# Attention in a two-layer hybrid block: probabilities times values as float32 matmuls, two heads side by side in the array's columns, row sums added up on GpSimd

## The chip, the cores and the metric

The kernel runs on one core of one Trainium2 chip. The metric is device time of one execution in microseconds, as the median of several runs. The core has five engines that take their instructions in order: TensorE (PE, with its weight loads shown apart as PEld), VectorE (DVE), ScalarE (ACT), GpSimd (POOL) and SyncE (SP, which issues the DMA transfers here).

## The reference

Two layers work on 512 latent tokens and 256 context tokens of width 1024. The first mixes tokens by multi-head latent attention with 16 heads, the second by a Hyena convolution; each is followed by a gated ConvFFN. Only the output of the latent tokens is returned, so the context matters as keys and values of the attention. The part that the change touches is, in the reference:

```python
    def one_block(qblk):
        s = jnp.einsum('bqhd,bkhd->bhqk', qblk, k).astype(F32) * scale
        p = jax.nn.softmax(s, axis=-1).astype(v.dtype)
        return jnp.einsum('bhqk,bkhd->bqhd', p, v)
```

All data are float32. There are 512 queries and 768 keys, 96 numbers in a query or key of a head and 64 in a value.

## The kernel before

Matmuls are made as products of split numbers. A float32 number is cut into a high part, rounded to the type float32r, and a low part, the rest; `mm3` (L137 to L139) adds three float32r matmuls, high by high, high by low and low by high. Weights are split on arrival by ACT (L129) and DVE (L130). A few small products use float32 operands as they are: the column sums and broadcasts of the norms (L247, L296), and the modulation rows of `Mods.rows` (L168). The latter puts four matmuls with 32 stationary columns each into four column groups of the array, by writing to partitions 0, 32, 64 and 96 of one PSUM tile `modp`.

The attention works on pairs of heads: `p` is the pair, `kt` a block of 128 of the 768 keys (six blocks), `b` the head of the pair. All is held with keys on the partitions and the 512 queries along the row.

- `s_step` makes the scores of a block with three float32r matmuls (tile `s`), then the exponentials twice, as float32r (`ph`) and as float32 (`pf`), on ACT; the difference `pl` is made on POOL or DVE by turns (L754, L756).
- `v_step` multiplies by the values. `split_v` has cut the values `vf` into `vh` (64 columns and two of ones, so that the row sums of the exponentials come out as rows 64 and 65) and `vl`. Three matmuls for each head and block, L768, L769 and L771, go to a PSUM tile for each head, `po0` and `po1`. After the last block ACT copies sums and results out (`sm`, `ou`), and the sums go by DMA through DRAM, a reciprocal on DVE (L781) and a broadcast back as `rb`; `normalize` multiplies (L793) and splits the result into `oh` and `ol` for the projection (`pj`).
- `side` weaves the preparation of the next pair in between: keys (`pk`), queries (`pq`, `rot`), and the largest scores, which are found by a float32r product of the high parts (`sm` written by L728, 384 columns, into the one tile that DVE's maximum L730 reads) and turned into a row by four small matmuls with one stationary column (`mr`, L735).

What stands in the code is not the order in which an engine runs it: the framework's scheduler orders each engine's instructions when the program is built, so that a matmul of `side` may stand between two matmuls of one `v_step`.

Of the kernel before, what the change touches and what calls it, by code (L numbers as in the profile page):

```python
# [17 lines left out]
P = 128  # L18
D = 1024
NC = D // P  # L20
T = 512
TC = 256
TK = T + TC
HEADS = 16
# [6 lines left out]
ATT_SCALE = 1.0 / math.sqrt(96.0)  # L31
# [26 lines left out]
def hybrid_kernel(ctx, tc, A, out):  # L58
    nc = tc.nc
    dma = nc.sync.dma_start  # L60
    act = nc.scalar.activation
    stt = nc.vector.scalar_tensor_tensor
    vtt = nc.vector.tensor_tensor
    vts = nc.vector.tensor_scalar
    mm = nc.tensor.matmul
# [40 lines left out]
    ones = gp.tile([P, P], F32, name="ones")  # L106
# [241 lines left out]
                              hh[:, j, c], hl[:, j, c], self.tmp, self.n)  # L348
            return hh, hl

# [1 line left out]
    def sin_of(ps, b, f, pool, outt, n):  # L352
        a = pool.tile([P, T], F32, tag="ff", name="sa", bufs=2)[:, :n]
        r = pool.tile([P, T], F32, tag="ff", name="sn", bufs=2)[:, :n]
# [106 lines left out]
                        if kt:  # L461
                            between()

# [182 lines left out]
    def attention(ab, L):  # L646
        at, cosq, sinq, cqh, cql = (L[n] for n in ("at", "cos", "sin", "cqh", "cql"))
        kb = L["kb"] + [(ab.tile([P, TK], F32R, name=f"kh{i}"), ab.tile([P, TK], F32R, name=f"kl{i}")) for i in (2, 3)]
        qb = [(ab.tile([P, T], F32R, name=f"qh{i}"), ab.tile([P, T], F32R, name=f"ql{i}")) for i in range(4)]
        vb = [(ab.tile([P, 6, 2, 66], F32R, name=f"vh{i}"), ab.tile([P, 6, 2, 64], F32R, name=f"vl{i}")) for i in range(2)]  # L650
        for vh, _ in vb:
            for b in range(2):
                nc.vector.tensor_copy(out=vh[:, :, b, 64:66], in_=ones[:, 0:12].rearrange("p (k o) -> p k o", o=2))

        wq = {0: tuple(wcols(w, 4, 384) for w in L["wuq"])}

# [7 lines left out]
        vf = {}  # L664

        def load_v(p):
            vf[p] = ab.tile([P, 6, 2, 64], F32, tag="vf", name="vf", bufs=1)
            dma(out=vf[p].rearrange("p k b d -> p k (b d)"), in_=vst[p // 4][p % 4])

        def split_v(p):  # L670
            vh, vl = vb[p % 2]
            nc.scalar.copy(out=vh[:, :, :, 0:64], in_=vf[p])
            nc.gpsimd.tensor_tensor(out=vl, in0=vf[p], in1=vh[:, :, :, 0:64], op=ALU.subtract)

        def gemm_q(g, r):
            pe = pst("pq")
# [4 lines left out]

        def prod_rope(g, meanwhile=None):
            pe = gemm_q(g, 0)
            ph = ab.tile([P, T], F32R, tag="ph", name="rph", bufs=5)
            pl = ab.tile([P, T], F32R, tag="pl", name="rpl", bufs=5)
# [6 lines left out]
            sb = ab.tile([P, T], F32, tag="ou", name="rsb", bufs=1)  # L692
# [45 lines left out]
        pts = {}  # L738

        def s_step(h, kt):  # L740
            kh, kl = kb[h % 4]
            qh, ql = qb[h % 4]
            ks = slice(kt * P, kt * P + P)
            s = pst("s")
            mm(s, lhsT=kh[0:97, ks], rhs=qh[0:97], start=True, stop=False)
            mm(s, lhsT=kh[0:96, ks], rhs=ql[0:96], start=False, stop=False)
            mm(s, lhsT=kl[0:96, ks], rhs=qh[0:96], start=False, stop=True)
            pf = at.tile([P, T], F32, tag="wv", name="pf", bufs=4)
            ph = ab.tile([P, T], F32R, tag="ph", name="ph", bufs=5)
            pl = ab.tile([P, T], F32R, tag="pl", name="pl", bufs=5)  # L750
# [10 lines left out]
        def v_step(p, kt):  # L761
            if kt == 0:
                pos[p] = (pso("po0"), pso("po1"))
            P2 = [pts.pop((2 * p + b, kt)) for b in range(2)]
            vh, vl = vb[p % 2]
            f, l = kt == 0, kt == 5
# [3 lines left out]
            for b in range(2):  # L770
                mm(pos[p][b][:66], lhsT=vh[:, kt, b, :], rhs=P2[b][1], start=False, stop=l)  # L771
            if l:
                ou = ab.tile([P, T], F32, tag="ou", name="ou", bufs=1)
                sm = at.tile([P, T], F32, tag="wv", name="sm", bufs=4)
                for b in range(2):
                    nc.scalar.copy(out=sm[32 * b:32 * b + 2], in_=pos[p][b][64:66])
                    dma(out=rst[0][p][b:b + 1, :], in_=sm[32 * b:32 * b + 1])
                    nc.scalar.copy(out=ou[64 * b:64 * b + 64], in_=pos[p][b][:64])
# [9 lines left out]
        norm = []  # L788

        def normalize():  # L790
            while norm:
# [7 lines left out]
        prod_rope(0, lambda: prod_q(0))  # L799
        for t in (1, 2):  # L800
            L["prod_v"](1, t)
        split_v(0)
# [19 lines left out]
        def side(n, i):  # L822
            if i == 11 and n % 2 and n + 1 < NP:
                prod_rope((n + 1) // 2)
            if n >= NP:
                return
            if i == 0:
                put_rope(n)
                if n > 1:
                    prod_k(n, 0, kb, L)  # L830
            elif i == 1 and n > 1:
                prod_k(n, 1, kb, L)
            elif i == 2:
                if n > 1:
                    prod_q(n)
                if n % 2 and n // 2 + 1 < 4:
                    load_wq(n // 2 + 1)
            elif 2 < i < 11:
                max_step(2 * n + (i - 3) // 4, (i - 3) % 4)
                if i == 6 or i == 10:  # L840
                    max_row(2 * n + (i == 10))
                if i == 9:
                    split_v(n)
                    if n + 1 < NP:
                        load_v(n + 1)

        pend = []
        for p in range(NP):
            for kt in range(6):
                for b in range(2):  # L850
                    s_step(2 * p + b, kt)
                    side(p + 1, 2 * kt + b)
                    if b == 1 and len(pend) == 2:
                        v_step(*pend.pop(0))
                if kt == 2:
                    normalize()
                pend.append((p, kt))
        while pend:
            v_step(*pend.pop(0))
        normalize()  # L860
        return oh, ol

# [1 line left out]
    def project(x, rh, rl, wname, gl, nm, mid, extra, bname=None):  # L864
        bg = None
        if bname:
# [71 lines left out]
                        if half:  # L938
                            nm.add(x[:, q, c], h)

# [1 line left out]
    def hyena(hh, hl):  # L942
        with tc.tile_pool(name="hy", bufs=1, side="left", reuse_waits="tile") as hy:
            yf = hy.tile([P, NC, T], F32, name="yf")
# [152 lines left out]
            split_y(range(6, 8))  # L1097
        return yh, yl

# [1 line left out]
    atx = ExitStack()  # L1101
    oh, ol = mla()
    atx.close()
# [171 lines left out]
```

## Time and profile before

| | |
|---|---|
| time, median of 3 runs | 1461.13 us (1460.64 to 1461.48) |
| span of the profiled execution | 1459.7 us |
| PE busy in it | 1395.5 us (96%) |
| DVE, ACT, POOL busy | 975.7, 615.9, 205.8 us |
| mean granted clock of PE | 0.986 |

The span runs from the first to the last instruction on the core; the profiled execution's own time is not given apart from it, and the 1.4 us between its span and the median of the runs is what lies around a span. Matmuls are pipelined and the end of each is modelled, so a matmul's listed duration overlaps with the next one's; the time from one start to the next is what a matmul costs in a dense stretch. The attention, from the first exponentials to the start of the projection, lies at about 187 to 394 us.

### The profile page before, as it was taken

How to read it: one execution, taken by the hardware profiler on the slowest of the kernel's cores; microseconds unless marked ns; L12 is line 12 of the kernel's file. 1: busy time of each engine (PE TensorE's matmuls, PEld its weight loads, DVE VectorE, ACT ScalarE, POOL GpSimd, SP SyncE). 2: the span in 40 equal slices, each digit the busy share in tenths (PEclk: the TensorE clock that was granted, in tenths of full speed). 3: DMA queues.
4: the chain of work that ended last, by engine and by line, in shares of the span. 5: the costliest groups of instructions: out<-in, count | busy, mean ns of one | idle time of the engine just before them, and what ended most of it. 6: DMA issues, size and time to landing. Idle time of an engine off the chain costs nothing. (4 is left out here: it accounts for less than half of the span.)

```text
span 1459.7 us, 17476 instructions
## 1 busy us (share of the span) xinstructions
PE 1395.5 (96%) x6766; PEld 1111.5 (76%) x6766; DVE 975.7 (67%) x1471; ACT 615.9 (42%) x965; POOL 205.8 (14%) x168
## 2 busy tenths in 40 slices
PE   5899899999999999999999999999899999999997
PEld 2577677766688878787878987887798888888886
DVE  5875676677467877657764688889786653355545
ACT  5444478678724433224342352323344432234420
POOL 4401124323330000000001103331310000000011
PEclk9999999999999999999999999999999999999998
DMA  9672511113162754665523342122313223332121
GB/s 367 218 272 96 150 33 59 41 55 113 45 228 96 234 189 164 235 233 183 181 89 112 141 164 104 68 85 86 134 70 115 78 68 104 116 112 78 60 79 58
DMA packets 46670, 186.58 MB, mean 128 GB/s; under 512 B 5320, under 2 KB 17864, under 8 KB 32380
## 3 DMA queue, kind: packets, MB, share of 16 engines
q1 hardware_dynamic: 46588, 185.48, 37.0%
q8 instruction: 53, 0.87, 0.2%
q14 instruction: 29, 0.24, 0.0%
HBM read 171.29 MB, written 11.60 MB: 125 GB/s over the span
## 5 line engine op out<-in xcount | busy, mean ns | idle before, releaser
L129 ACT CAST wh<-wr 128x1024 fp32r<-128x1024 f32 (+2 forms) x209 | 195.4, 955 | 180.8 <-PE dn L138 89.0
L130 DVE TENSOR_TENSOR wl<-wr,wh 128x1024 fp32r<-128x1024 f32 (+2 forms) x209 | 242.4, 1175 | 24.3 <-ACT wh L129 21.2
L267 POOL TENSOR_TENSOR sqa<-sqa,sq 128x512 f32<-128x512 f32 (+1 forms) x42 | 58.2, 1386 | 837.1 <-ACT sq L265 836.1
L139 PE MATMUL dn<-gh,wl 128*128 128x512 f32 (+1 forms) x396 | 146.8, 371 | 0.0
L137 PE MATMUL dn<-gh,wh 128*128 128x512 f32 (+1 forms) x396 | 146.7, 372 | 0.0
L138 PE MATMUL dn<-gl,wh 128*128 128x512 f32 (+1 forms) x396 | 146.3, 369 | 0.0
L318 DVE SCALAR_TENSOR_TENSOR z<-ua,vec,z 128x511 f32<-128x511 f32 x44 | 33.0, 750 | 109.9 <-ACT z L317 109.8
L934 DVE SCALAR_TENSOR_TENSOR x<-dn,modc,x 128x512 f32<-128x512 f32 (+1 forms) x36 | 24.9, 691 | 109.4 <-PE dn L139 109.4
L317 ACT ACTIVATE z<-ua,vec 128x512 f32<-128x512 f32 x44 | 34.3, 780 | 149.2 <-PE ua L139 149.2
L137 PEld LDWEIGHTS dn<-gh,wh 128*128 128x128 f32 x396 | 74.4, 188 | 15.6 <-ACT wh L129 0.8
L138 PEld LDWEIGHTS dn<-gl,wh 128*128 128x128 f32 x396 | 74.5, 188 | 14.3
L139 PEld LDWEIGHTS dn<-gh,wl 128*128 128x128 f32 x396 | 74.4, 188 | 13.9
L137 PE MATMUL hz<-hyh,wh 128*128 128x512 f32 (+1 forms) x224 | 82.2, 368 | 0.0
L139 PE MATMUL hz<-hyh,wl 128*128 128x512 f32 (+1 forms) x224 | 81.9, 366 | 0.0
L754 POOL TENSOR_TENSOR pl<-pf,ph 128x512 fp32r<-128x512 f32 x48 | 63.0, 1318 | 133.3 <-ACT pf L752 132.0
L138 PE MATMUL hz<-hyl,wh 128*128 128x512 f32 (+1 forms) x224 | 81.7, 365 | 0.0
L901 ACT ACTIVATE sg<-z 128x512 f32<-128x512 f32 x44 | 27.8, 633 | 109.6 <-DVE z L319 104.4
L137 PE MATMUL ua<-hf1h,wh 128*128 128x512 f32 (+1 forms) x192 | 72.5, 378 | 1.1 <-ACT hf1h L307 1.1
L138 PE MATMUL ua<-hf0l,wh 128*128 128x512 f32 (+1 forms) x192 | 72.9, 380 | 0.4 <-DVE hf0l L308 0.4
L137 PE MATMUL ua<-hf0h,wh 128*128 128x512 f32 (+1 forms) x192 | 73.1, 381 | 0.0
L138 PE MATMUL ua<-hf1l,wh 128*128 128x512 f32 (+1 forms) x192 | 72.6, 378 | 0.5 <-DVE hf1l L308 0.5
L139 PE MATMUL ug<-hf0h,wl 128*128 128x512 f32 (+1 forms) x192 | 73.0, 380 | 0.0
(388 smaller groups left out, 3572.7 us busy)
## 6 DMA issues: line engine op xcount, KB each, us to landing
wr<-in_wup SPq DMA_DIRECT2D x44, 1024.0 KB
mw<-in_modw SPq DMA_DIRECT2D x40, 1024.0 KB
wr<-in_wdn SPq DMA_DIRECT2D x32, 704.0 KB
wr<-in_win SPq DMA_DIRECT2D x12, 1024.0 KB
mw<-in_modw SPq DMA_DIRECT2D x16, 512.0 KB
fspec<-fs SPq DMA_DIRECT2D x16, 256.0 KB
wr<-in_wo SPq DMA_DIRECT2D x4, 1024.0 KB
fq<-fspec SPq DMA_DIRECT2D x8, 512.0 KB
```

The source lines that it names most:

```text
L129: nc.scalar.copy(out=wh[:, c], in_=wr[:, c])
L130: vtt(out=wl[:, c], in0=wr[:, c], in1=wh[:, c], op=ALU.subtract)
L137: mm(ps, lhsT=ah, rhs=bh, start=first, stop=False)
L138: mm(ps, lhsT=ah, rhs=bl, start=False, stop=False)
L139: return mm(ps, lhsT=al, rhs=bh, start=False, stop=last)
L267: nc.gpsimd.tensor_tensor(out=acc, in0=acc, in1=sq, op=ALU.add)
L317: act(out=z, in_=p, func=AF.Identity, bias=b, scale=w1)
L318: stt(out=z[:, 1:T], in0=p[:, 0:T - 1], scalar=w0, in1=z[:, 1:T], op0=ALU.mult, op1=ALU.add)
L754: nc.gpsimd.tensor_tensor(out=pl, in0=pf, in1=ph, op=ALU.subtract)
L901: act(out=sg, in_=zs[1], func=AF.Silu)
L934: i = stt(out=x[:, q, c], in0=job[0][:, c], scalar=mcol(l, 5, q), in1=x[:, q, c], op0=ALU.mult, op1=ALU.add)
```

## The change

The values are no longer split and the exponentials are made once, as float32. `v_step` is called for two blocks at a time, and makes one float32 matmul for each head and block: the first head of a pair writes to partitions 0 to 63 of one PSUM tile `po`, the second to 64 to 127, which puts them in the two halves of the array's columns. The row sums no longer come from columns of ones: the exponentials of a head are added up into a tile `acc` (on POOL, the last four on DVE), and `row_sums` multiplies it by a float32 tile of ones, 32 columns for each head of the pair. Buffers change too: `pf` has a tag of its own with eight, `vf` and `ou` have two.

```diff
-        def split_v(p):
-            vh, vl = vb[p % 2]
-            nc.scalar.copy(out=vh[:, :, :, 0:64], in_=vf[p])
-            nc.gpsimd.tensor_tensor(out=vl, in0=vf[p], in1=vh[:, :, :, 0:64], op=ALU.subtract)
...
-            act(out=ph, in_=s, func=AF.Exp, scale=ATT_SCALE)
             act(out=pf, in_=s, func=AF.Exp, scale=ATT_SCALE)
-            if (h + kt) % 2 == 0:
-                nc.gpsimd.tensor_tensor(out=pl, in0=pf, in1=ph, op=ALU.subtract)
+            pts[h, kt] = pf
+            if kt == 0:
+                return
+            if kt == 1:
+                accs[h] = ab.tile([P, T], F32, tag="acc", name="acc", bufs=4)
+                prev = pts[h, 0]
             else:
-                vtt(out=pl, in0=pf, in1=ph, op=ALU.subtract)
-            pts[h, kt] = (ph, pl)
+                prev = accs[h]
+            add = vtt if h >= HEADS - 2 and kt > 3 else nc.gpsimd.tensor_tensor
+            add(out=accs[h], in0=prev, in1=pf, op=ALU.add)
...
-            for b in range(2):
-                mm(pos[p][b][:66], lhsT=vh[:, kt, b, :], rhs=P2[b][0], start=f, stop=False)
-                mm(pos[p][b][:64], lhsT=vl[:, kt, b, :], rhs=P2[b][0], start=False, stop=False)
-            for b in range(2):
-                mm(pos[p][b][:66], lhsT=vh[:, kt, b, :], rhs=P2[b][1], start=False, stop=l)
...
+        def v_step(p, kts):
+            if kts[0] == 0:
+                pos[p] = pso("po")
+            for kt in kts:
+                for b in range(2):
+                    mm(pos[p][64 * b:64 * b + 64], lhsT=vf[p][:, kt, b, :], rhs=pts.pop((2 * p + b, kt)),
+                       start=kt == 0, stop=kt == 5)
+            if kts[-1] == 5:
+                ou = ab.tile([P, T], F32, tag="ou", name="ou", bufs=2)
+                nc.scalar.copy(out=ou, in_=pos.pop(p))
+                ends.append((p, ou))
...
+        def row_sums():
+            while ends:
+                p, ou = ends.pop(0)
+                rsum = pst("rsum")
+                for b in range(2):
+                    mm(rsum[32 * b:32 * b + 32], lhsT=ones[:, 0:32], rhs=accs.pop(2 * p + b), start=True, stop=True)
                 sm = at.tile([P, T], F32, tag="wv", name="sm", bufs=4)
+                nc.scalar.copy(out=sm[0:64], in_=rsum[0:64])
...
-                if kt == 2:
+                if kt % 2 == 0 and pend:
+                    v_step(*pend.pop(0))
+                if kt == 1:
+                    row_sums()
+                if kt == 4:
                     normalize()
-                pend.append((p, kt))
+                if kt % 2:
+                    pend.append((p, (kt - 1, kt)))
```

Where the instructions come to stand on PE is the scheduler's doing. The first place is the product of one step with the values in the third pair of heads; a row is a line of the code, the tile written from the tiles read, and columns by row length. Before, the six matmuls of a block stand so, with a product of `side` among them:

```order
L768 MATMUL po_1664<-ph,vh_1354 66x512
L728 MATMUL sm<-kh_612,qh_1346 128x384 x2
L769 MATMUL po_1664<-ph,vl_1355 64x512
L768 MATMUL po_1665<-ph,vh_1354 66x512
L769 MATMUL po_1665<-ph,vl_1355 64x512
L771 MATMUL po_1664<-pl,vh_1354 66x512
L771 MATMUL po_1665<-pl,vh_1354 66x512
```

In the changed kernel the four matmuls of two blocks stand so (heads alternate from one to the next; line 719 is `side`'s product, 736 to 738 the scores):

```order
L738 MATMUL s<-qh_1352,kl_1345 128x512
L759 MATMUL po<-pf,vf 64x512 x3
L719 MATMUL sm<-kh_612,qh_1346 128x384 x2
L759 MATMUL po<-pf,vf 64x512
L736 MATMUL s<-qh_1350,kh_1342 128x512
```

The four are cut into a run of three and a run of one by a product that fills all 128 columns. The whole order has 45 runs of `po`: 2 of four matmuls, 22 of three, 1 of two and 20 of one, 96 matmuls in all.

The second place is the row sums of the same pair, which did not stand on PE before:

```order
L738 MATMUL s<-qh_1352,kl_1345 128x512
L773 MATMUL rsum<-acc,ones 32x512
L719 MATMUL sm<-kh_612,qh_1346 128x384 x2
L773 MATMUL rsum<-acc,ones 32x512
L736 MATMUL s<-qh_1350,kh_1342 128x512
```

The two heads' sums are parted by the same kind of product. There are 14 runs of `rsum`: 12 of one matmul and 2 of two, the last of them right behind the last run of `po`.

## Rows read from the trace of the kernel before

**Rows 1.** The page: PE's busy time; GpSimd's float32 addition.

```profile
PE 1395.5 (96%) x6766; PEld 1111.5 (76%) x6766; DVE 975.7 (67%) x1471; ACT 615.9 (42%) x965; POOL 205.8 (14%) x168
...
L267 POOL TENSOR_TENSOR sqa<-sqa,sq 128x512 f32<-128x512 f32 (+1 forms) x42 | 58.2, 1386 | 837.1 <-ACT sq L265 836.1
```

**Rows 2.** Windows view, attention: busy us (instructions) of PE, PEld, DVE, ACT, POOL; PE clock.

```profile
190.00:394.00 204.00, 197.67 (x899) 140.44 (x899) 137.58 (x180) 155.83 (x289) 72.10 (x53) 1.00 0.19 61
```

**Rows 3.** Waits of PE in that window: us in total, times, longest.

```profile
PE mr L735 <- DVE mx L730: 1.9, 3, 0.8
PE po L768 <- ACT ou L778: 1.0, 2, 0.7
PE sm L728 <- DVE mx L730: 0.9, 2, 0.7
PE pq L137 <- ACT pf L752: 0.9, 1, 0.9
```

**Rows 4.** Timeline of PE in a product with the values: start us, duration us.

```profile
260.16 0.40 PE L768 MATMUL po<-ph,vh 128*66 128x512 f32 x1
260.39 0.39 PE L769 MATMUL po<-ph,vl 128*64 128x512 f32 x1
...
260.86 0.39 PE L769 MATMUL po<-ph,vl 128*64 128x512 f32 x1
```

**Rows 5.** Groups in the window of rows 2: busy us, mean ns.

```profile
L754 POOL TENSOR_TENSOR pl<-pf,ph 128x512 fp32r<-128x512 f32 x47 | 61.8, 1319 | 126.7 <-ACT pf L752 125.4 <-PE po L769 1.3
...
L751 ACT ACTIVATE ph<-s 128x512 fp32r<-128x512 f32 x91 | 55.1, 606 | 21.9 <-PE s L747 14.9 <-PE po L769 5.8
```

**Rows 6.** Timeline of PE around four modulation matmuls in four column groups.

```profile
45.31 0.39 PE L137 MATMUL fps<-w3h,hs 128*128 128x512 f32 x1
45.63 1.06 PE L168 MATMUL modp<-mw,sc 128*32 128x512 f32 x8
46.62 0.50 PE L138 MATMUL fps<-w3l,hs 128*128 128x512 f32 x1
46.96 0.39 PE L139 MATMUL fps<-w3h,hs 128*128 128x512 f32 x1
```

**Rows 7.** The same around eight of them.

```profile
93.37 0.39 PE L139 MATMUL kv<-hxh,wl 128*128 128x512 f32 x1
93.69 1.92 PE L168 MATMUL modp<-mw,sc 128*32 128x512 f32 x16
95.54 0.39 PE L137 MATMUL kv<-ch,wh 128*128 128x256 f32 x1
95.76 0.28 PE L138 MATMUL kv<-cl,wh 128*128 128x256 f32 x1
```

**Rows 8.** The same around a single one, in the first column group.

```profile
28.12 0.39 PE L139 MATMUL fps<-w3h,hs 128*128 128x512 f32 x1
28.44 1.04 PE L168 MATMUL modp<-mw,sc 128*32 128x512 f32 x2
29.42 0.50 PE L137 MATMUL fa<-pqh,dfteh 128*128 128x512 f32 x1
29.76 0.39 PE L138 MATMUL fa<-pql,dfteh 128*128 128x512 f32 x1
```

**Rows 9.** Timeline of PE around a float32 matmul over all columns.

```profile
149.96 1.02 PE L296 MATMUL bq<-dg,ones 128*128 128x512 f32 x2
150.41 0.80 PE L138 MATMUL pv<-wuv,ckh 128*128 128x512 f32 x1
151.05 0.40 PE L139 MATMUL pv<-wuv,ckl 128*128 128x512 f32 x1
```

**Rows 10.** Timeline around the last pair's row sums, the way through DRAM.

```profile
393.94 1.18 ACT L776 COPY sm<-po 2x512 f32<-2x512 f32 x2 [1.14 <-PE po L771]
...
397.92 0.54 DVE L781 RECIPROCAL rs<-rs 16x64 f32<-16x64 f32 x1 [4.06 <-DMA rs<-rst]
...
403.69 0.69 DVE L793 TENSOR_TENSOR ou<-ou,rb 128x512 f32<-128x512 f32 x1 [5.24 <-DMA rb<-rst]
```

More of the change, by code (lines that the diff above doesn't have):

```diff
@@ L649, in attention @@
         qb = [(ab.tile([P, T], F32R, name=f"qh{i}"), ab.tile([P, T], F32R, name=f"ql{i}")) for i in range(4)]
-        vb = [(ab.tile([P, 6, 2, 66], F32R, name=f"vh{i}"), ab.tile([P, 6, 2, 64], F32R, name=f"vl{i}")) for i in range(2)]
-        for vh, _ in vb:
-            for b in range(2):
-                nc.vector.tensor_copy(out=vh[:, :, b, 64:66], in_=ones[:, 0:12].rearrange("p (k o) -> p k o", o=2))
         wq = {0: tuple(wcols(w, 4, 384) for w in L["wuq"])}
@@ L666, in load_v @@
         def load_v(p):
-            vf[p] = ab.tile([P, 6, 2, 64], F32, tag="vf", name="vf", bufs=1)
+            vf[p] = ab.tile([P, 6, 2, 64], F32, tag="vf", name="vf", bufs=2)
             dma(out=vf[p].rearrange("p k b d -> p k (b d)"), in_=vst[p // 4][p % 4])
-        def split_v(p):
-            vh, vl = vb[p % 2]
-            nc.scalar.copy(out=vh[:, :, :, 0:64], in_=vf[p])
-            nc.gpsimd.tensor_tensor(out=vl, in0=vf[p], in1=vh[:, :, :, 0:64], op=ALU.subtract)
         def gemm_q(g, r):
@@ L683, in prod_rope @@
             pe = gemm_q(g, 0)
-            ph = ab.tile([P, T], F32R, tag="ph", name="rph", bufs=5)
-            pl = ab.tile([P, T], F32R, tag="pl", name="rpl", bufs=5)
+            ph = ab.tile([P, T], F32R, tag="ph", name="rph", bufs=1)
+            pl = ab.tile([P, T], F32R, tag="pl", name="rpl", bufs=1)
             split_ps(pe, ph, pl)
@@ L691, in prod_rope @@
             mm(rot, lhsT=perm_r, rhs=pl, start=False, stop=True)
-            sb = ab.tile([P, T], F32, tag="ou", name="rsb", bufs=1)
+            sb = ab.tile([P, T], F32, tag="ou", name="rsb", bufs=2)
             qt = ab.tile([P, T], F32, tag="rb", name="rqt", bufs=1)
@@ L736, in max_row @@
             act(out=qb[h % 4][0][96:97], in_=mr[0:1, :], func=AF.Copy, scale=-1.0)
-        pts = {}
+        pts, accs = {}, {}
         def s_step(h, kt):
@@ L747, in s_step @@
             mm(s, lhsT=kl[0:96, ks], rhs=qh[0:96], start=False, stop=True)
-            pf = at.tile([P, T], F32, tag="wv", name="pf", bufs=4)
-            ph = ab.tile([P, T], F32R, tag="ph", name="ph", bufs=5)
-            pl = ab.tile([P, T], F32R, tag="pl", name="pl", bufs=5)
-            act(out=ph, in_=s, func=AF.Exp, scale=ATT_SCALE)
+            pf = ab.tile([P, T], F32, tag="pf", name="pf", bufs=8)
             act(out=pf, in_=s, func=AF.Exp, scale=ATT_SCALE)
-            if (h + kt) % 2 == 0:
-                nc.gpsimd.tensor_tensor(out=pl, in0=pf, in1=ph, op=ALU.subtract)
-            else:
-                vtt(out=pl, in0=pf, in1=ph, op=ALU.subtract)
@@ L757, in s_step @@
-            pts[h, kt] = (ph, pl)
+            pts[h, kt] = pf
[4 more added lines that the diff above has]
+                prev = pts[h, 0]
+            else:
+                prev = accs[h]
+            add = vtt if h >= HEADS - 2 and kt > 3 else nc.gpsimd.tensor_tensor
+            add(out=accs[h], in0=prev, in1=pf, op=ALU.add)
         pos = {}
[L761 to L766, printed above, removed]
-            for b in range(2):
-                mm(pos[p][b][:66], lhsT=vh[:, kt, b, :], rhs=P2[b][0], start=f, stop=False)
-                mm(pos[p][b][:64], lhsT=vl[:, kt, b, :], rhs=P2[b][0], start=False, stop=False)
-            for b in range(2):
-                mm(pos[p][b][:66], lhsT=vh[:, kt, b, :], rhs=P2[b][1], start=False, stop=l)
-            if l:
-                ou = ab.tile([P, T], F32, tag="ou", name="ou", bufs=1)
+        def v_step(p, kts):
[9 more added lines that the diff above has]
+                ends.append((p, ou))
@@ L774, in v_step @@
+        ends, norm = [], []
+        def row_sums():
[4 more added lines that the diff above has]
+                    mm(rsum[32 * b:32 * b + 32], lhsT=ones[:, 0:32], rhs=accs.pop(2 * p + b), start=True, stop=True)
                 sm = at.tile([P, T], F32, tag="wv", name="sm", bufs=4)
+                nc.scalar.copy(out=sm[0:64], in_=rsum[0:64])
                 for b in range(2):
-                    nc.scalar.copy(out=sm[32 * b:32 * b + 2], in_=pos[p][b][64:66])
@@ L777, in v_step @@
                     dma(out=rst[0][p][b:b + 1, :], in_=sm[32 * b:32 * b + 1])
-                    nc.scalar.copy(out=ou[64 * b:64 * b + 64], in_=pos[p][b][:64])
                 rs = ab.tile([16, 64], F32, tag="rs", name="rs", bufs=1)
@@ L786, in v_step @@
                 norm.append((p, ou, rb))
-        norm = []
         def normalize():
@@ L801, in attention @@
             L["prod_v"](1, t)
-        split_v(0)
         for h in range(2):
@@ L841, in side @@
                     max_row(2 * n + (i == 10))
[L842 to L845, printed above, removed]
+                if i == 9 and n + 1 < NP:
+                    load_v(n + 1)
         pend = []
@@ L852, in attention @@
                     side(p + 1, 2 * kt + b)
-                    if b == 1 and len(pend) == 2:
-                        v_step(*pend.pop(0))
-                if kt == 2:
+                if kt % 2 == 0 and pend:
[3 more added lines that the diff above has]
+                if kt == 4:
                     normalize()
-                pend.append((p, kt))
-        while pend:
-            v_step(*pend.pop(0))
+                if kt % 2:
+                    pend.append((p, (kt - 1, kt)))
+        v_step(*pend.pop(0))
+        row_sums()
         normalize()
```

## The prediction

> **What bounds the kernel now.** I began with the page's busy times: PE is busy for 1395.5 of 1459.7 us [rows 1]. That figure alone can mislead, because listed matmuls overlap, so I asked the windows view for the stretch of the attention. There PE shows 197.7 of 204.0 us, at the full clock, while ACT shows 155.8, DVE 137.6 and POOL 72.1 [rows 2]. 6.3 us are left in which PE shows no work. The waits say where most of that is: 1.9 and 0.9 us for DVE's maxima, 1.0 us of `po` for ACT's copy out of the bank, 0.9 us of `pq` for an exponential [rows 3], 4.7 us together. So in this stage time is what PE's own list of matmuls takes, and an instruction taken from another engine returns only its part of those few microseconds. The change must therefore be priced by what it does to PE.
>
> **PE: what goes.** The product with the values has 3 matmuls for each of 16 heads and 6 blocks, 288 in all. From one start to the next they take (260.86 - 260.16) / 3 = 0.233 us [rows 4]. 288 x 0.233 = 67.1 us leave PE.
>
> **PE: what comes.** No product with the values in float32 is in this trace, but the parts of its price are. A float32 matmul over all columns leaves two records, and 1.09 us pass from the first one's start to that of the second float32r matmul behind it [rows 9]. Take 0.233 off for the matmul between, and 0.86 us remain: two slots of 0.43 us for a row of 512, and nothing for changing to float32 and back. Whether matmuls in different column groups share slots is seen in the modulation rows. Four of them (eight records) take 46.62 - 45.63 = 0.99 us from their start to the next matmul [rows 6], two slots and a little; eight (two in each group) take 95.54 - 93.69 = 1.85 us [rows 7], four slots. So groups do run side by side. A run of the new matmuls thus costs two slots for every matmul in its fuller half of the columns.
>
> But there is a turnaround at both ends of a run. From the float32r matmul ahead of the four to the second one behind them are 46.96 - 45.31 = 1.65 us [rows 6]; two float32r steps of 0.233 would have been there anyway, so the run cost 1.18 us. Two slots are 0.86, and 0.32 us go into entering and leaving. A single one, two records in the first column group, gives 29.76 - 28.12 - 0.47 = 1.17 us [rows 8], as much as four; the eight 95.76 - 93.37 - 0.35 = 2.04 us [rows 7] (0.35 for one step of 512 and one of half the columns, taken as half of 0.233). So a run of two slots costs 1.18 us and one of four 2.04 us.
>
> Now the order decides. If each `v_step` stayed whole, 24 runs of four would cost 49.0 us, a gain of 18 on 67.1 before the sums. The scheduler has cut them: the order has 2 runs of four and 22 of three, all with two matmuls in the fuller half, so 24 runs at 2.04 us, and 1 of two and 20 of one at 1.18 us. The row sums add 14 runs of two slots, also 1.18 us. 24 x 2.04 + 35 x 1.18 = 49.0 + 41.3 = 90.3 us, less 0.3 because the last run of sums follows one of `po` with no turnaround between. **PE's list grows by 90.0 - 67.1 = 22.9 us.** Of the 90.0, 166 slots of 0.43 are 71.4 and 58 turnarounds 18.6.
>
> The sure bounds of this term: with no turnaround at all it is 71.4 - 67.1 = +4.3 us. If the two halves did not share slots, all 112 matmuls would pay two slots, 96.3 + 18.6 - 67.1 = +47.8 us. I take the value of the modulation rows, because in them are float32 matmuls placed among the columns, at the same length and in the same kind of surroundings.
>
> The Trainium skill bears on this in its page "TensorE: Matmul & The Clock Gate" (Part 3, what overlaps and what doesn't): matmuls stay in program order in start and end. Read for the two records of each matmul, that would make a staircase, in which the second head's first record begins only with the first head's second one. Runs of two and of four would then take one slot more, 5 of them here, 2 us in all. The sixteen records of rows 7 in four slots show no such staircase, so I add nothing. The page "TensorEngine Tiling (Array Packing)" (Key Properties) says that changing the tiling mode drains the array. Rows 6 to 8 agree with 0.32 us a visit; the step of 0.233 us between 66 and 64 columns [rows 4] shows that a narrower stationary operand alone does not do it.
>
> **The other engines.** ACT loses one of two exponentials (96 at 606 ns, 58 us [rows 5]) and half of the copies out of `po`; DVE loses 48 subtractions. POOL loses 48 subtractions at 1319 ns [rows 5] and gains 76 additions, at 1386 ns by the norm's float32 addition [rows 1]: 105 us in some 210, or 10 additions and 14 us in a pair, which lasts about 26 (204.0 us [rows 2] hold nearly eight). It comes nearer to its limit but not to it; the exponentials that it adds wait in eight buffers, of which six are in use at most. What covers the additions is PE's next block and a half before `row_sums`; without it each pair would show up to 2.8 us, two additions.
>
> What PE gets back from this lies in rows 3. The 1.0 us for the bank goes, since a pair now takes one of two banks and before took both. The 0.9 us of `pq` goes, since a bank of scores is free after one exponential. Of the 2.8 us for DVE's maxima I take three quarters, because DVE loses 48 subtractions in the same queue: 2.1 us. Together 4.0 us; the ends are 0 and the whole 6.3 us of idle time.
>
> **New waits that I cost at nothing.** The load of `vf` stands later on SP, behind PE's last use of the older buffer; behind it queue copies of the next pair's rope rows and the sums, but it is needed a whole pair later. The way of the sums begins one block after `po` ends, and `normalize` moves from block 2 to block 4. That way takes 397.92 - 393.94 = 4.0 us to the reciprocal and 403.69 - 397.92 = 5.8 us more to the multiplication [rows 10]. On DVE four maxima stand ahead of the reciprocal and three between it and the multiplication; eight maxima in a pair's 26 us are 3.2 us apart, and where they stand dense perhaps half of that, 6.4 and 4.8 us of cover, about enough. If it is late, DVE stands at the head of its queue, the maxima behind it wait, and then PE's `sm` and `mr`. At the end of the attention the sums begin one run later and need one copy fewer; I take that as even.
>
> **Sum.** Against the profiled span: 1459.7 + 22.9 - 4.0 = 1478.6 us. With the 1.4 us that lie around a span in the median of the runs, **1480 us**, 1.3% slower.
>
> **Rivals.** (a) *No turnaround for halves of the columns.* What speaks for it is rows 4, where narrow float32r matmuls turn freely; against it, rows 8, where one narrow float32 matmul in the first group pays in full. Then +4.3 us less the 4.0 to 6.3 given back: 1459 to 1461.5 us, and with slots of 0.41 us (1.85 us of rows 7 less 0.2 at its end, over four) some 3 us less, 1456 to 1458. This is the side on which the kernel is not slower. It decides when a turnaround costs less than about 0.05 us, since 58 of them then no longer pass 3 us. (b) *The halves do not share slots*: +47.8 - 4.0, 1505 us. For it: rows 6 and 7 have four groups of 32, not halves. Against it: each of those four groups has a moving row of its own, as the halves would, and they share. (c) *The sums come late.* DVE waits at the reciprocal or the multiplication, and PE for the maxima behind. At 2 us in each of seven pairs that is 14 us on top, 1494 us. For it: the way is as long as its cover; against it: DVE has more room than before. (d) *The turnaround is partly hidden*, at half its price for the single runs: 32 runs x 0.16 = 5 us less, 1475 us; I count it in the forecast's own range.
>
> **How the numbers follow.** A measurement of this kernel can tell about 0.2%, 2.9 us, from no change. Chances: the forecast with (d) 0.73, own range 1471 to 1487 us (the 6.3 us given back and a third of the turnarounds gone, to nothing given back and 0.05 us more for each turnaround and late sums in part); (a) 0.13, of it 0.06 faster, 0.05 the same and 0.02 slower; (b) 0.05; (c) 0.09. Slower has 0.73 + 0.05 + 0.09 + 0.02 = 0.89. The range that leaves out no more than 2 in 10 goes from 1463, past most of (a), to 1494, through (c).
>
> **What the changed profile would show.** Starts of `po` records: two heads within some hundredths of a microsecond, slots of 0.43 us; about 0.3 us lost between full-width neighbours and a run; 45 runs of `po` and 14 of `rsum`. The attention longer by 15 to 23 us with PE still its bound, ACT near half busy, POOL near half, no `po` waiting for `ou`. Stages after it as long as before. The prediction is wrong if the runs turn without loss, if heads follow one another, or if PE's largest wait is for DVE behind `rb`.

## The result, and the profile after

The changed kernel takes 1473.34 us in the median of 4 runs (1472.18 to 1477.55), the kernel before 1460.99 us (1460.64 to 1461.48). The ratio is 1.009, with a 95% interval of 1.0072 to 1.0108: slower, as forecast, by 12 us where 19 were forecast.

The page of the changed kernel, its busy times and the additions on GpSimd, answers [rows 1]:

```profile
PE 1412.3 (96%) x6702; PEld 1086.9 (74%) x6702; DVE 952.1 (65%) x1423; ACT 556.6 (38%) x845; POOL 223.6 (15%) x188
...
L750 POOL TENSOR_TENSOR acc<-acc,pf 128x512 f32<-128x512 f32 x60 | 77.4, 1306 | 49.6 <-ACT pf L740 48.5
```

The windows view of the attention (columns as in [rows 2]), and the waits of PE in it (as in [rows 3]):

```profile
190.00:405.00 215.00, 214.52 (x834) 117.31 (x834) 111.25 (x136) 101.05 (x175) 92.82 (x72) 1.00 0.18 57
```

```profile
PE mr L726 <- DVE mx L721: 0.5, 1, 0.5
```

PE now shows work in all but 0.5 of 215 us, at the full clock, and one wait is left in this window. ACT and POOL come to about half, as forecast; an addition on POOL took 1306 ns where the forecast used 1386, a mean over two shapes.

How long the attention is, shows in the start of the first score and of the first matmul of the projection behind it. Timeline of PE, start and duration in us, first of the kernel before:

```profile
182.39 0.39 PE L745 MATMUL s<-qh,kh 97*128 97x512 f32 x1
...
393.92 0.39 PE L137 MATMUL pj<-oh,wh 128*128 128x512 f32 x1
```

and of the changed kernel:

```profile
180.74 0.39 PE L736 MATMUL s<-qh,kh 97*128 97x512 f32 x1
...
405.53 0.50 PE L137 MATMUL pj<-oh,wh 128*128 128x512 f32 x1
```

211.53 us have become 224.79, 13.3 more. From the projection to the end of the span (1459.7 and 1471.4 us) it is 1065.8 and 1065.9, as long as before. Ahead of the attention 1.65 us are gone. The change takes the first `split_v` out of that stretch, and the experiments below edit nothing more there; yet in the kernels of this study the first score starts anywhere from 180.5 to 186.0 us, so I ascribe nothing to that.

The new runs are these. Timeline of PE in the changed kernel, a run of one matmul (x2 records) and one of three (x6):

```profile
234.48 0.34 PE L139 MATMUL pk<-ckh,wl 128*128 128x384 f32 x1
234.75 1.07 PE L759 MATMUL po<-pf,vf 128*64 128x512 f32 x2
235.75 0.50 PE L736 MATMUL s<-qh,kh 97*128 97x512 f32 x1
236.09 0.40 PE L737 MATMUL s<-ql,kh 96*128 96x512 f32 x1
...
237.44 0.33 PE L139 MATMUL pk<-ckh,wl 128*128 128x384 f32 x1
237.70 1.93 PE L759 MATMUL po<-pf,vf 128*64 128x512 f32 x6
239.56 0.50 PE L736 MATMUL s<-qh,kh 97*128 97x512 f32 x1
239.90 0.40 PE L737 MATMUL s<-ql,kh 96*128 96x512 f32 x1
```

What a run costs is read as in the prediction: from the start of the matmul ahead to that of the second one behind, less those two steps (0.233 us, and 0.177 for the 384 columns of `pk`). The single one costs 236.09 - 234.48 - 0.41 = 1.20 us, the three 239.90 - 237.44 - 0.41 = 2.05 us. The forecast had 1.18 and 2.04.

With this rule the whole attention can be booked. The other 642 matmuls (scores, maxima, projections, rotations) are the same in both kernels; by their steps they take 129.2 us. The product with the values took 67.1 us before, the runs of `po` and `rsum` take 91.6 us now. One of these runs has a wait in its price. It stands ahead of the window shown above:

```profile
185.77 1.93 PE L759 MATMUL po<-pf,vf 128*64 128x512 f32 x6
188.54 0.62 PE L719 MATMUL sm<-kh,qh 96*128 96x384 f32 x2 [0.84 <-DVE mx L721]
```

The `sm` behind this run waits for DVE's maximum, so that the run costs 2.96 us by the rule where its like cost 2.06. Without these 0.9 us the list is 90.7 us. What is left over is waiting and small delays: 211.5 - 129.2 - 67.1 = 15.2 us before, 224.8 - 129.2 - 90.7 = 4.9 us now. So the list of PE grew by 23.6 us, and 10.3 us were given back. In the experiments below, the price of runs is always by the rule, with waits at their ends in it; the changed kernel's 91.6 us, and the 4.0 us left over beside them, are what to compare with.

### The profile page after: what moved, and what is told of

Same layout as the page of the kernel before. It is cut to its first block, busy times and chain, and to the rows that moved or that the text cites. A ratio compares the mean times of both kernels' runs of the same rounds, so it can differ in the third digit from the quotient of the medians.

```text
span 1471.4 us, 17226 instructions
## 1 busy us (share of the span) xinstructions
PE 1412.3 (96%) x6702; PEld 1086.9 (74%) x6702; DVE 952.1 (65%) x1423; ACT 556.6 (38%) x845; POOL 223.6 (15%) x188
## 5 line engine op out<-in xcount | busy, mean ns | idle before, releaser
L130 DVE TENSOR_TENSOR wl<-wr,wh 128x1024 fp32r<-128x1024 f32 (+2 forms) x209 | 247.4, 1199 | 30.0 <-ACT wh L129 27.4
L721 DVE TENSOR_REDUCE mx<-sm 128x1 fp32r<-128x768 f32 x56 | 53.6, 956 | 55.1 <-PE sm L719 54.7
L740 ACT ACTIVATE pf<-s 128x512 f32<-128x512 f32 x96 | 56.8, 597 | 79.9 <-PE s L738 78.4
L750 POOL TENSOR_TENSOR acc<-acc,pf 128x512 f32<-128x512 f32 x60 | 77.4, 1306 | 49.6 <-ACT pf L740 48.5
```

The lines of the kernel that those rows point to most:

```text
L130: vtt(out=wl[:, c], in0=wr[:, c], in1=wh[:, c], op=ALU.subtract)
L721: nc.vector.reduce_max(out=mxs[h][:, qt:qt + 1], in_=b2[:, :, :384], axis=AX.XY)
L750: add(out=accs[h], in0=prev, in1=pf, op=ALU.add)
```

## The experiments

**Does the price of a run explain the time?** The theory says that a run costs two slots for each matmul in its fuller half, and a turnaround. If so, fewer cuts must pay. The first try held each group of four and each pair of sums together in a critical section of the scheduler:

```
...
+            with tc.tile_critical():
                 for kt in kts:
                     for b in range(2):
                         mm(pos[p][64 * b:64 * b + 64], ...
...
+                with tc.tile_critical():
                     for b in range(2):
                         mm(rsum[32 * b:32 * b + 32], ...
```

> The changed kernel with each group of four products with the values, and each pair of row sums, issued as one uninterrupted run: 23 runs of four slots, 7 of two and a last one of both, where the changed kernel has 24 and 35. Theory (a run costs two slots of 0.43 us for each matmul in its fuller half of the columns, and 0.32 us of turnaround): 112 slots in place of 166 and 31 turnarounds in place of 58, 54 x 0.43 + 27 x 0.32 = 32 us less than the changed kernel, about 1441 us, so faster than the kernel before by some 20 us. Rival 1 (a cut costs only its turnaround): 27 x 0.32 = 9 us less, about 1464.5 us. Rival 2 (whole runs hold up the scores and the maxima behind them, and PE then waits for exponentials): a third or more of the 32 us comes back as waits, 1452 us or above.

> As the kernel with whole runs, but the row sums stay as the scheduler cuts them: 6 of the pairs of sums are two single runs. Theory: 6 x 1.18 = 7 us more than with the sums whole, about 1448 us. Rival (a narrow run of sums between full-width matmuls is hidden or costs only a turnaround): 0 to 2 us more, about 1441 to 1443 us.

Measured: 1536.1 us with both sections (ratio to the kernel before 1.0513, 1.049 to 1.0535), 1526.3 us with the one around `po` alone (1.0422, 1.0385 to 1.0458). The theory's 1441 and 1448 us and the first rivals are missed by far. The time lies in the range of the second rival of the first kernel (1452 us or above), but the waits of PE in that kernel (185 to 400 us) name another reason than exponentials held up:

```profile
PE po L760 <- POOL acc L750: 11.5, 7, 2.8
PE po L760 <- DMA rb<-rst: 5.3, 2, 2.8
...
PE rsum L775 <- DMA wr<-in_wo: 4.6, 1, 4.6
```

A product with the values reads neither `acc` nor `rb`, and the row sums have nothing to do with a weight `wr`. The section puts a wait for unrelated work ahead of itself. A run of it in the timeline:

```profile
231.95 1.94 PE L760 MATMUL po<-pf,vf 128*64 128x512 f32 x8 [1.41 <-POOL acc L750]
```

1.41 us stand ahead of it; the run itself has its four slots in 1.94 us. So these two kernels tell what the sections cost, not what whole runs cost, and the forecast for them said nothing of that wait. They also lost clock: over the attention of the first (182 to 468 us) PE shows 225.9 of 286 us and a granted clock of 0.88, so part of it at the lower level, where the changed kernel has 1.00 throughout.

**Do the halves share their slots?** The kernel with whole runs, with both heads in the first 64 columns, each in a bank of its own:

```
-                        mm(pos[p][64 * b:64 * b + 64], ...
+                        mm(pos[p][b][:64], ...
```

> As the kernel with whole runs, but both heads of a pair take the first 64 columns, each with a bank of its own (and one copy more out of the banks for each pair). Theory (matmuls share slots because they stand in different columns): a run of four takes eight slots in place of four, 24 x 4 x 0.43 = 41 us more than the kernel with whole runs, about 1482 us. Rival (what makes the pairs cheap is only that the four follow each other without a turnaround): 0 to 4 us more, about 1441 to 1445 us.

Measured: 1582.3 us (1.0823, 1.0803 to 1.0843), 46 us above the kernel with both sections. The sections are in both, and the timeline shows the rest at once:

```profile
233.97 3.65 PE L760 MATMUL po<-pf,vf 128*64 128x512 f32 x8 [0.71 <-DMA rst<-sm]
```

The same eight records take 3.65 us where they took 1.94. By the rule above the runs of the attention cost 174.1 us in this kernel and 131.4 in the other (with some 50 us of delay ahead of the runs in each, and some runs at the lower clock), 42.7 us apart; 41 were expected. At the full clock a run of four takes 2.03 us there and 3.73 us here (medians, from its start to the next matmul), and 24 x 1.70 is 41 us as well. Sharing by columns is shown.

**Fewer and more cuts, without sections.** Now the four matmuls of a step, and the two of a pair's row sums, are written in reverse, so that the one whose probabilities come last stands first and the others are ready behind it:

```
-            for kt in kts:
-                for b in range(2):
+            for kt in kts[::-1]:
+                for b in (1, 0):
...
-                       start=kt == 0, stop=kt == 5)
+                       start=kt == 1, stop=kt == 4)
```

> The changed kernel with the four matmuls of a step written in reverse, so that the one whose probabilities come last stands first; the scheduler then leaves 41 runs of two slots and 9 of four or more in place of 35 and 24. Theory: 41 x 1.18 + 8 x 2.05 + 3.0 = 68 us of runs in place of 91, 23 to 24 us less than the changed kernel, about 1450 us. Rival (a cut costs its turnaround alone): 50 runs in place of 59, 9 x 0.32 = 3 us less, 1470 us.

Measured: 1457.0 us, 16 less than the changed kernel, and faster than the kernel before (0.9958, 0.9943 to 0.9974). The pairs stand in the timeline like this:

```profile
220.60 1.08 PE L759 MATMUL po<-pf,vf 128*64 128x512 f32 x4
221.61 0.62 PE L719 MATMUL sm<-kh,qh 96*128 96x384 f32 x2
222.16 1.08 PE L759 MATMUL po<-pf,vf 128*64 128x512 f32 x4
```

A pair (x4) lasts as long as a single one did (x2, 1.07 us). The runs of the attention cost 70.1 us in place of 91.6, the attention takes 205.0 us in place of 224.8. In the whole time 7 of the expected 23 us are missing: 2 in the runs (two waits at their ends, 0.9 us each), 1.7 in more waiting elsewhere, 4 in the stretch ahead of the attention, whose spread was told above, less 0.3 behind it. The rival, 1470 us, is refuted.

The other way: the products and sums get the scheduler's high priority.

```
+            with tc.high_priority():
                 for kt in kts:
```

> The changed kernel with the products and the sums given the scheduler's high priority: they are issued as soon as their probabilities are there, mostly one by one. 87 runs of two slots and 3 of four. Theory: 87 x 1.18 + 3 x 2.05 = 109 us of runs in place of 91, 17 us more than the changed kernel, about 1490 us. Rival 1 (the second head's matmul is hidden under the work around it, so single runs cost half a turnaround less): about 1476 us. Rival 2 (a cut costs its turnaround alone, 31 x 0.32): 1483 us.

Measured: 1511.2 us (1.034, 1.0321 to 1.0359), 38 us above the changed kernel where 17 were expected. Both rivals, which made a cut cheaper, are refuted. Two thirds of the surplus stand in the runs: 123.0 us where 109 were expected. A pair of it on PE,

```profile
260.20 1.66 PE L760 MATMUL po<-pf,vf 128*64 128x512 f32 x4
```

and on ACT the exponential of its second head:

```profile
260.14 0.60 ACT L740 ACTIVATE pf<-s 128x512 f32<-128x512 f32 x1 [0.68 <-PE s L738]
```

The pair lasts 1.66 us in place of 1.08. The exponential ends at 260.74, more than half a microsecond after the first head's start, and the second head begins 0.05 us later: PE waits inside the run. Nine pairs cost 1.8 to 2.0 us in place of 1.2, and several single runs 1.3 to 1.4, most of them with a short wait ahead. The price by slots and turnarounds is a lower bound that holds when the operands are there.

**Whole runs by order.** The same whole runs as with the sections, by edges that fix an instruction's place in PE's queue and wait for nothing:

```
+    def whole(first):
+        for i in log[first - NB:first]:
+            behind(log[first], i)
+        for i, j in zip(log[first + 1:], log[first:]):
+            behind(i, j)
+        fence[:] = log[-1:]
```

> The changed kernel with the same whole runs as in the kernel with critical sections, but made by order alone: edges that fix the place of an instruction in PE's queue and wait for nothing. 23 runs of four slots, 7 of two and a last one of both. Theory (the loss in the two kernels with critical sections is the wait for all other engines that such a section puts ahead of itself; a whole run costs 2.04 us and a pair of sums 1.18): the runs take 58 us in place of 91, so about 33 us less than the changed kernel, 1440 us, and faster than the kernel before by some 20 us. Rival 1 (whole runs themselves make PE wait for exponentials and maxima behind them): half of it or more comes back, 1456 us or above. Rival 2 (a cut costs its turnaround alone, 27 x 0.32): 1464 us.

Measured: 1477.8 us (1.0107, 1.0092 to 1.0122). That is 58 us less than with the sections, so the sections were indeed most of that loss; but the forecast of 1440 is wrong, and the first rival right. The runs do cost less, 64.9 us, but 32.7 us are left over beside them, where the changed kernel has 4.0. 20 of them are idle time. Another part is slower matmuls: the granted clock was at its lower level for 14 us of the attention (0.97 in the mean). Its waits of PE:

```profile
PE sm L73 <- DVE mx L740: 15.3, 16, 2.7
PE rot L73 <- ACT rph L651: 2.0, 3, 0.7
```

The maxima have one buffer in PSUM (`b2`, bufs=1), so each pair of `sm` waits for DVE's reduction of the one before. With every run fixed in place, maxima that the scheduler spread between scores stand packed next to a run:

```profile
229.29 0.51 PE L73 MATMUL sm<-kh,qh 96*128 96x384 f32 x2
230.86 0.61 PE L73 MATMUL sm<-kh,qh 96*128 96x384 f32 x2 [1.05 <-DVE mx L740]
```

What the length of the runs adds to that is not separated here; in the reversed kernel, with 8 runs of four, 5.7 us were left over in all.

The next kernel therefore left the maxima free and fixed the rest, on top of the reversed order; it also fixes a run behind the 4 matmuls written ahead of it, where the last kernel took 24 (`NB`):

```
...
+        if free:
+            return i
...
```

> As the reversed kernel, with order edges added between the runs and the matmuls of scores and projections alone; those of the maxima stay free to move. 27 runs of two slots, 15 of four and the last one, in place of 41, 8 and the last. Theory: 27 x 1.18 + 15 x 2.05 + 3.0 = 65.6 us of runs in place of 67.8, about 2 us less than the reversed kernel, 1455 us, faster than the kernel before by some 6 us. Rival (any fixed place makes PE wait for DVE's maxima, as it did where all runs were whole): 1460 us or above.

Measured: 1461.2 us, no different from the kernel before (0.9991, 0.998 to 1.0003), and so not better than the reversed kernel. The rival is right in its time, 1460 us or above, but not in its reason. The runs cost 69.4 us, 0.7 less, where 2 less were expected; one run of four took 3.70 us, while the granted clock was at its lower level for 3.4 us. 10.4 us are left over against 5.7. PE's idle time for DVE's maxima is 1.4 us, 0.3 more than in the reversed kernel; what is new are waits for ACT:

```profile
PE s L73 <- ACT qh L748: 1.4, 4, 0.9
PE rot L73 <- ACT rph L653: 1.2, 3, 0.7
```

**What gave PE time back?** The forecast took 4.0 us, half of it for the subtractions that leave DVE. Two kernels without the change's matmuls try that alone. The first one leaves out the second exponential and the subtractions of the kernel before, the second one the subtractions only:

```
-            act(out=pf, in_=s, func=AF.Exp, scale=ATT_SCALE)
-            if (h + kt) % 2 == 0:
-                nc.gpsimd.tensor_tensor(out=pl, in0=pf, in1=ph, op=ALU.subtract)
-            else:
-                vtt(out=pl, in0=pf, in1=ph, op=ALU.subtract)
-            pts[h, kt] = (ph, pl)
+            pts[h, kt] = (ph, ph)
```

> The kernel before with its 288 float32r matmuls, but with one exponential in each step and no subtraction: the low part of the probabilities is replaced by the high part (so the output leaves out their low part). PE's list is that of the kernel before; ACT, DVE and POOL are relieved much as in the changed kernel. Theory (the idle time of the windows view understates what PE loses to waits, since each listed matmul lasts longer than its step; the starts show 13.8 us of it in the attention): 8 to 12 us faster than before, 1449 to 1453 us. Rival 1 (the forecast's reading: at most the 6.3 us in which PE shows no work, likely 4): 1455 to 1457 us. Rival 2 (the relief of these engines gives nothing, the waits went with the bank and the order): 1459 to 1461 us.

> The kernel before with both exponentials and no subtraction: the low part of the probabilities is replaced by the high part (so the output leaves out their low part). With one exponential less as well it was 5.9 us faster. Theory 1 (PE waited for maxima behind the subtractions in DVE's queue): all of it stays, 1455 to 1457 us. Theory 2 (PE waited for the second exponential, which holds the bank of the scores and ACT's copies): 1459 to 1461 us.

Measured: 1455.5 us for the first (0.9965, 0.9952 to 0.9978), 1461.6 us for the second, no difference (1.0001, 0.9989 to 1.0013). The windows view of the second one's attention:

```profile
190.00:394.00 204.00, 198.65 (x902) 141.07 (x901) 103.18 (x133) 154.13 (x289) 10.20 (x6) 1.00 0.20 61
```

DVE fell from 137.6 to 103.2 us and POOL from 72.1 to 10.2, and the attention takes 210.6 us in place of 211.5: that relief is worth nothing that can be measured. Theory 2 comes nearest there. Without the second exponential as well it takes 205.5 us, which is what the first rival of that kernel said, not the theory. So in the order of the kernel before the second exponential costs 5 to 6 us, although the waits of [rows 3] name DVE for 2.8 of 4.7.

Then the reverse, in the changed kernel: first both put back as work that nothing uses, then the exponential alone.

```
+            ph = at.tile([P, T], F32, tag="wv", name="ph", bufs=4)
+            act(out=ph, in_=s, func=AF.Exp, scale=ATT_SCALE)
+            sub = nc.gpsimd.tensor_tensor if (h + kt) % 2 == 0 else vtt
+            sub(out=ph, in0=pf, in1=ph, op=ALU.subtract)
```

> The changed kernel with the second exponential and the subtraction put back as work that nothing uses (96 exponentials on ACT, 48 subtractions each on DVE and POOL). Its runs on PE come out at 94 us in place of 91, 2.4 us more by the count. Theory (what PE got back came from the relief of these engines): the waits return as well, 6 to 10 us on top, 1482 to 1486 us. Rival 1 (what PE got back came from the bank and the order): 1475 to 1477 us. Rival 2 (POOL, now with 108 additions and subtractions at 1.3 us in each two pairs, becomes the bound): 1490 us or above.

> The changed kernel with the second exponential alone put back, as work that nothing uses (96 on ACT); no subtraction. The scheduler leaves 40 runs of two slots, 20 of four and the last, 91 us as in the changed kernel. Theory (what PE got back beyond the bank came from the second exponential, which holds the bank of the scores for 0.6 us more): about 6 us more than the changed kernel, 1477 to 1482 us. Rival 1 (ACT has room for it, and the waits went with the bank and the order): 1472 to 1475 us. Rival 2 (the second exponential is what cost most of the 26 us when exponential and subtraction were put back together): 1488 us or above.

Measured: 1499.1 us with both (1.0256, 1.0221 to 1.029), and 1474.3 us with the exponential alone (1.0092, 1.0075 to 1.0109), the same as the changed kernel. The windows view of the latter:

```profile
190.00:405.00 215.00, 214.59 (x828) 116.61 (x830) 109.83 (x136) 141.57 (x265) 96.27 (x75) 1.00 0.19 58
```

ACT is back at 141.6 of 215 us, and PE waits no more than without it. My theory fell here; the rival is right. In the changed order, with one bank for a pair, the second exponential is covered. So the 26 us of the other kernel are not the second exponential's. They lie in the range of the second rival (1490 us or above), but POOL is busy for 174.7 of 253 us there, so it does not bound the attention throughout. Waits of PE in that kernel:

```profile
PE mr L726 <- DVE mx L721: 12.5, 5, 8.7
PE rsum L777 <- DVE acc L754: 5.0, 1, 5.0
```

The longest, in the timelines of PE, DVE and POOL:

```profile
193.62 1.07 PE L763 MATMUL po<-pf,vf 128*64 128x512 f32 x2
203.37 0.26 PE L726 MATMUL mr<-ident_r,mx 128*1 128x128 f32 x1 [8.69 <-DVE mx L721]
```

```profile
191.65 10.80 DVE L744 TENSOR_TENSOR ph<-pf,ph 128x512 f32<-128x512 f32 x2
202.37 0.95 DVE L721 TENSOR_REDUCE mx<-sm 128x1 fp32r<-128x768 f32 x1
```

```profile
191.44 1.30 POOL L744 TENSOR_TENSOR ph<-pf,ph 128x512 f32<-128x512 f32 x1
192.70 3.72 POOL L754 TENSOR_TENSOR acc<-acc,pf 128x512 f32<-128x512 f32 x3
...
200.03 1.27 POOL L754 TENSOR_TENSOR acc<-acc,pf 128x512 f32<-128x512 f32 x1
```

Two subtractions on DVE last 10.8 us together, where one takes 1.1 us in the median of this kernel; POOL works without a gap all the while. The maximum behind them comes late, and PE waits 8.7 us. This happened once, in a profiled execution of 1505.1 us (the four runs lie between 1494.7 and 1505.1). The granted clock was at its lower level from 199.1 to 209.3 us, so the matmuls behind the wait were slower as well. What makes up the rest of the 26 us is not taken apart here.

**The sums on GpSimd or on DVE.** All additions on DVE:

```
-            add = vtt if h >= HEADS - 2 and kt > 3 else nc.gpsimd.tensor_tensor
+            add = vtt
```

> The changed kernel with all 80 additions on DVE, none on GpSimd. The scheduler then leaves 35 runs of two slots, 21 of four and the last, 87 us in place of 91. Theory (the additions are off the path on GpSimd, and DVE has room for them at about 0.6 us each): about 1469 us by the count, 1467 to 1472. Rival 1 (on DVE they stand ahead of the maxima, for which PE waits): 6 us or more on top, 1475 us or above. Rival 2 (on GpSimd the sums were on the path after all): below 1466 us.

Measured: 1478.7 us (1.0117, 1.0097 to 1.0137). Its runs cost 89.5 us, 2 less, its waiting 8.1 us, 4 more, so the attention (226.8 us) is 2 us longer. The rest stands ahead of the attention and behind it, where nothing was edited: the profiled execution took 1483.3 us (the four runs lie between 1476.1 and 1483.3), and its granted clock was at the lower level for 6.8 us just ahead of the attention. DVE is at 149.1 of 215 us in the windows view:

```profile
190.00:405.00 215.00, 212.12 (x822) 116.73 (x821) 149.08 (x209) 100.22 (x174) 0.00 (x0) 0.99 0.19 58
```

The first rival comes nearest, with 4 in place of its 6 us. That GpSimd is the better place for the additions, by those 2 us, is what one profile shows; that the sums were on the path there (below 1466 us) is refuted.

## Why the prediction was right, and where it was off

*PE's list.* 90.7 us of runs, or 91.6 with the wait behind one of them, where 90.0 were forecast, in the forecast number: 45 runs of `po` (one of them with the last sums) and 13 of sums alone. The prices from the modulation rows [rows 6 to 8] held to 0.02 us for a different operand, a different width and halves in place of quarters. The other kernels of this study book the same way: 1.2 us for two slots and 2.06 for four in each, at the full clock and unless an operand is late.

*The rivals.* (a), no turnaround, would have shown runs of 0.86 us: refuted. (b), no sharing, is what the kernel with both heads in the same columns shows, 42.7 us of runs more than its pair: refuted for the changed kernel. (c), late sums, did not come: no wait of PE in the attention stands behind `rb`, and DVE waited for it once, for 0.2 us. (d), a partly hidden turnaround for single runs, gives 1475 us, close to the measured time, but for a reason that is not there: the single run costs 1.20 us in full. That agreement is by chance.

*What PE gets back.* This is the step that failed: "Together 4.0 us; the ends are 0 and the whole 6.3 us of idle time." It was 10.3 us. The upper end was wrong, not only the choice inside it. In the starts of the kernel before there are 24 places in the attention where the next matmul comes more than 0.12 us later than a step; they sum to 10.2 us, and their idle time to 6.3 us, just the idle time of [rows 2]. The 3.9 us between are about 24 times 0.16 us, by which a matmul's listed 0.40 us outlast its step of 0.233. One of them, PE in the kernel before:

```profile
221.22 0.39 PE L769 MATMUL po<-ph,vl 128*64 128x512 f32 x1
222.16 0.22 PE L735 MATMUL mr<-ident_r,mx 128*1 128x128 f32 x1 [0.55 <-DVE mx L730]
```

0.94 us from start to start, where 0.23 would do, cost 0.71 us; the view says 0.55. In the changed kernel two such places are left, of 0.65 us and of the 0.9 us behind the run at 185.77. I had written that listed matmuls overlap, and then took the idle time as a bound all the same. The other 5 us before (3.4 now) are delays of some hundredths each.

*Why it came back.* The forecast's reason, 48 subtractions less in DVE's queue, is refuted: without the subtractions the kernel before is no faster. Its second exponential is worth 5 to 6 us there, and nothing in the changed order. So either the relief of ACT or the new order removes those 5 to 6 us. What of the remaining 4 to 5 belongs to the second bank that a pair now finds free, what to the order, and what to PE's slower pace of 28 us a pair, which gives the other engines more time, the runs don't separate.

*The sum.* Against 1480 us: runs +0.7, given back -6.3, the stretch ahead of the attention -1.65, behind it +0.1, around the span +0.5 (1.9 in place of 1.4). That makes 1473.3.

The change itself is sound in its core and loses by its cuts: with its matmuls in reverse order it beats the kernel before by 0.4% (0.26 to 0.57). What the turnaround is made of shows in part in the kernel before. A float32 matmul over all columns stands there among float32r ones:

```profile
55.98 0.39 PE L139 MATMUL fb<-pqh,dftel 128*128 128x512 f32 x1
56.22 1.02 PE L296 MATMUL bc<-dg,ones 128*128 128x512 f32 x2
56.67 0.79 PE L137 MATMUL fo<-pqh,dfto0h 128*128 128x512 f32 x1
57.30 0.39 PE L138 MATMUL fo<-pql,dfto0h 128*128 128x512 f32 x1
```

By the rule for runs it costs 57.30 - 55.98 - 0.47 = 0.85 us, two slots and no turnaround; the one of [rows 9], with the matmul ahead of it at 149.73, costs 0.86 us. So the change from float32r to float32 alone cost nothing. Nor did float32r matmuls of 64 columns, always the first ones [rows 4]. Only float32 matmuls in a part of the columns paid 0.32 to 0.34 us; whether float32r ones in the second half would pay is not tested.

## What to carry to other kernels

Before replacing many full-width matmuls by narrow ones, count the runs in the order that the scheduler really leaves, since a matmul alone in its half costs as much as two side by side; write first the one whose operand comes last. Take an engine's lost time from the starts of its instructions, not from the idle time between listed ends. And test the engine that a wait names by taking work away from it: here 48 subtractions less on DVE gave nothing back.

## What the runs showed of the hardware

In the kernel with exponential and subtraction put back, a subtraction on DVE with two operands in SBUF took 10.2 of the 10.8 us shown above, while POOL ran eight operations of two operands one behind the other, and ended 0.55 us after the end of the last of them. The shortest of its like takes 0.66 us. The Trainium skill says in its page "SBUF — State Buffer" (SBUF: two separate sides) that the two engines share a pair of ports as an exclusive lock for a whole instruction, and the other one blocks. The trace agrees with a block, here through eight instructions. It is not what always happens when POOL works without a gap. Later in the same execution, in the timelines of DVE and POOL:

```profile
277.24 0.78 DVE L744 TENSOR_TENSOR ph<-pf,ph 128x512 f32<-128x512 f32 x1 [0.39 <-ACT ph L742]
```

```profile
276.18 4.68 POOL L754 TENSOR_TENSOR acc<-acc,pf 128x512 f32<-128x512 f32 x3
```

There the subtraction ended 0.55 us after the first of POOL's three additions, and the second addition took 1.73 us where the first took 1.29. Every other subtraction on DVE in this kernel took 1.74 us or less, in spite of stretches of nine and more operations on POOL without a gap. Why the block held once through eight of them stays open.

Two float32 matmuls in the two halves share slots only as far as they are in time together: where the second started 0.59 us late, in the pair of the kernel with high priority that is shown above, the run was longer by the same 0.59 us.
